# Second norm of a hybrid encoder layer: its small products a quarter of a block later in TensorE's order

## The chip, the cores and the metric

The kernel runs on one core of one Trainium2 chip, as one program. The metric is the device time of the execution in microseconds; the figure for a kernel is the median of its runs. The profile is of one further execution, taken by the hardware profiler. The engines are named as in the profile: PE is TensorE (its matmuls are called products here), PEld its weight loads, DVE is VectorE, ACT ScalarE, POOL GpSimd, SP SyncE, whose queue issues most DMAs.

## The reference

One encoder layer runs over two groups of tokens (2048 and 256) with the same weights; the width is 1024. The part that the change touches is in the second half of the layer: the output projection, its addition to the residual `x`, the second RMSNorm, and the start of the feed-forward part.

```python
def rmsnorm(x, w):
    y = x * lax.rsqrt(jnp.mean(x * x, axis=-1, keepdims=True) + EPS)
    return y * w

def encoder_layer(x, ...):
    h = rmsnorm(x, norm1_w)
    ... # mLSTM heads and attention heads on h @ w_in
    x = x + jnp.concatenate([m_out, a_out], axis=-1) @ w_out
    h = rmsnorm(x, norm2_w)
    u = centred_dwconv(h @ w_up, conv_w, conv_b)
    a, g = jnp.split(u, 2, axis=-1)
    return x + (jax.nn.silu(g) * a) @ w_down
```

A last RMSNorm follows. All is in float32.

## The kernel before, in words

The activations lie transposed on the chip: a tile has 128 of the 1024 channels in its partitions and tokens in its columns. A float32 operand is split in a high part and the rest (`fp32r`), and each product is made of three products of such parts.

The layer runs in phases. The first norm and the input projection come first; then the mLSTM heads, and with them and after them the attention heads. While the last attention blocks run, phase C (`phase_c`) makes the output projection, the residual and the second norm, block by block of 256 tokens. Phase U (`up_start`, `phase_u`) makes the first feed-forward product with a Strassen-like scheme of seven products, then the convolution and the gate; phase E the second feed-forward product and the last norm.

Phase C has nine blocks, taken in the order 0 to 6, 8, 7. A place in this order is called a turn here, turn 0 to turn 8. A turn has four quarters `z`, of 48 products each, and `mm` stops after each 12 of them (`k` is 0 to 3) so that a piece of attention can be put between: `phase_c` is a generator, and `run_both` steps it beside the attention's generator. The names in a turn are these:

- `cmx` is the projection's input, read from `mix_d` in HBM and split on ACT and DVE; `cx` is the residual, read from `xT` in HBM (L1060) into one of two buffers. `loads` issues both for the next turn after a turn's first quarter.
- `po` is a quarter's result in PSUM (two buffers); `post` adds it into `cx` on DVE (L1076), squares it on ACT (`csq`), and adds the squares up in `cacc` on POOL (L1082). `cacc` has one buffer.
- The norm's tail of a block stands in the next turn. `tail_a` folds `cacc` on POOL (L1085), then `rstd_cols` makes the small products of the sum with `ones` into `rs_c` (L135), takes the result on DVE (L138) and raises it to the power on POOL: `rcol_c` (L139). `tail_b` makes the small products of `rcol_c` with `ident` (L146), by which `rs_c` has a row of the factors in each partition, scales `cx` by `rs_c` on DVE (L1091) and stores the normed block to `n_d` in HBM (L1096).
- The last block's tail is `g.c_end`, called behind the first feed-forward unit's first two products.

The feed-forward part is done in two stretches of tokens, and a unit is two rows of 128 channels out of it. In the Strassen-like scheme the operands of the seven products are called "11", "21", "t2", "t1", "t3", "22" and "t4". "11", "21" and "22" (`n` in the rows) are quarters of the normed input, read from `n_d`; the `t` ones (`nt`) are differences of quarters, read from `n2t_d`. `n2_sums` makes these differences on POOL's queue, for a pair of channel tiles in two rounds (`rn`, two buffers): two loads from `n_d` (L1179), four subtractions (L1183), two stores to `n2t_d` (L1185). There are eight rounds for the first stretch of tokens; a pair is written into the code behind a quarter's `post`, from turn 5's second quarter on. `n2_load` (L1158 to L1160) loads an operand on SP in two pieces and splits it on ACT and DVE. `up_start` makes "11" into PSUM `pa` and "21" into `pb`; its function `rest` makes the other five. The weights `wu` and `wut` are split on ACT (L1221) and DVE.

What sets the order: each engine runs its own list, in the order that a scheduler gives at build time. While phase C runs beside attention, PE's list is in the order in which the code is written (`manual_schedule` for PE); the other engines' lists are sorted by the scheduler.

In the body, the remaining turns of phase C run without attention, with the loads of the first unit's operands put between:

```python
for _ in rest:
    if todo:
        todo.pop(0)()
for f in todo:
    f()
first = [up_start(g, s1, ..., ops, 0, NFC, rs)]
g.c_end()
```

Of the kernel before, what the change touches and what calls it, by code (L numbers as in the profile page):

```python
# [9 lines left out]
F32 = mybir.dt.float32  # L10
F32R = mybir.dt.float32r
AF = mybir.ActivationFunctionType
ALU = mybir.AluOpType
# [4 lines left out]
P = 128  # L18
D = 1024
NCC = D // P  # L20
# [6 lines left out]
NFC = FF // P  # L27
# [9 lines left out]
BT = 256  # L37
NB = T // BT
# [984 lines left out]
def phase_c(g, sn, sp, pp, wps):  # L1023

    nc = g.nc
    wo = ([], [])
    stage = []
    g.normed = set()  # L1030

    def weights(k, c):


        w = wps[k].tile([P, 2, 512], F32R, tag="w", name=f"wo{c}_{k}", bufs=WB)
        wo[k].append(w)
        if k == 0:
            t = g.raw.tile([P, 512], F32, tag="raw", name=f"ro{c}_{k}", bufs=2)
        else:
            if c % 4 == 0:  # L1040
                stage.append(sp.tile([P, 4, 512], F32, tag="x", name=f"ro{c}_{k}", bufs=2))
            t = stage[-1][:, c % 4]
        split(g, w[:, 0, :], w[:, 1, :], g.w_out[0, c * P:c * P + P, 512 * k:512 * k + 512], t)

    def loads(n, b):
        mx = []
        x = sp.tile([P, NCC, BT], F32, tag="x", name=f"cx{b}", bufs=2)
        for z in range(4):
            for o in range(2):
                c = 2 * z + o  # L1050
                if n and (n == 1 or n % 2 == 0):
                    m = sp.tile([P, 2, BT], F32R, tag="mx", name=f"cmx{b}_{c}", bufs=MXB)
                else:
                    m = sn.tile([P, 2, BT], F32R, tag="nT", name=f"cmx{b}_{c}", bufs=NTB)
                nc.sync.dma_start(f32(m[:, 1]), g.mix_d[b, :, c])
                nc.scalar.activation(m[:, 0], f32(m[:, 1]), AF.Copy)
                nc.vector.tensor_tensor(m[:, 1], f32(m[:, 1]), f32(m[:, 0]), ALU.subtract)  # L1057
                mx.append(m)
        for t in range(2):
            nc.sync.dma_start(x[:, :, t * P:(t + 1) * P], g.xT[2 * b + t])  # L1060
        return x, mx

    def mm(b, z, mx, po):

        for o in range(2):
            n = slice(((2 * z + o) % 4) * P, ((2 * z + o) % 4 + 1) * P)
            for c in range(NCC):
                for k, (a, h) in enumerate(((0, 0), (0, 1), (1, 0))):
                    nc.tensor.matmul(po[:, o], wo[z // 2][c][:, a, n], mx[c][:, h, :],  # L1069
                                     start=(c == 0 and k == 0), stop=(c == NCC - 1 and k == 2))  # L1070
                if c % 4 == 3:
                    yield

    def post(b, z, x, po, acc):
        xz = x[:, 2 * z:2 * z + 2]
        nc.vector.tensor_tensor(xz, po, xz, ALU.add)  # L1076
        if z % 2:
            g.st.dma_start(g.x1_d[:, 2 * z - 2:2 * z + 2, b * BT:(b + 1) * BT], x[:, 2 * z - 2:2 * z + 2])
        q = acc if z == 0 else sp.tile([P, 2, BT], F32, tag="sq", name=f"csq{b}_{z}", bufs=1)
        nc.scalar.activation(q, xz, AF.Square, scale=1.0 / 32.0)  # L1080
        if z:
            nc.gpsimd.tensor_tensor(acc, acc, q, ALU.add)  # L1082

    def tail_a(b, x, acc):
        nc.gpsimd.tensor_tensor(acc[:, 0], acc[:, 0], acc[:, 1], ALU.add)  # L1085
        return rstd_cols(g, sp, pp, [acc[:, 0]], BT, "r", f"c{b}")

    def tail_b(b, x, ps, r):
        r = rstd_rows(g, ps, r, BT)
        for z in range(NCC):  # L1090
            nc.vector.scalar_tensor_tensor(x[:, z], x[:, z], g.n2w[:, z:z + 1], r, ALU.mult, ALU.mult)  # L1091
            if z % 4 == 3:
                if b * BT < N2A:
                    g.st.dma_start(g.n2_d[0][:, z - 3:z + 1, b * BT:(b + 1) * BT], x[:, z - 3:z + 1])
                if b * BT >= N2B:
                    g.st.dma_start(g.n2_d[1][:, z - 3:z + 1, b * BT - N2B:(b + 1) * BT - N2B], x[:, z - 3:z + 1])  # L1096
        g.normed.add(b)

    for k in range(2):
        for c in range(NCC):  # L1100
            weights(k, c)
    sums = list(range(NCC // 2))

    order = (*range(NB - 2), NB - 1, NB - 2)
    nxt = loads(0, 0)
    yield None, C_LEAD
    prev = None
    for n, b in enumerate(order):
        x, mx = nxt
        for z in range(4):  # L1110
            if z == 1 and n + 1 < NB:
                yield 2 * order[n + 1], C_MM
                nxt = loads(n + 1, order[n + 1])
            po = pp.tile([P, 2, BT], F32, tag="po", name=f"po{b}_{z}")
            for k, _ in enumerate(mm(b, z, mx, po)):
                if z == 1 and k == 0 and prev is not None:
                    tail_b(*prev)
                if z < 3 or k < 3:
                    yield None, C_MM
            if z == 0:  # L1120
                if prev is not None:
                    prev = (*prev[0:2], *tail_a(*prev))
                acc = sp.tile([P, 2, BT], F32, tag="acc", name=f"cacc{b}", bufs=1)
            post(b, z, x, po, acc)
            if (n, z) > (5, 0) and sums:

                n2_sums(g, sp, 0, sums.pop(0), tag="rn", bufs=2)
        prev = (b, x, acc)

    def end():  # L1130
        tail_b(*prev[0:2], *tail_a(*prev))
    g.c_end = end

# [62 lines left out]
def banks(g, pool, name):  # L1198

    k = g.nbank = g.nbank + 1  # L1200
    return pool.tile([P, 2, 512], F32, tag=f"p{k % 2}", name=name, bufs=1)


def up_start(g, s1, bank, ops, b, jj, rs=None):


    nc = g.nc
    n = (DT[b + 1] - DT[b]) // 2
    m = n // 2
    nm = f"{b}_{jj}"  # L1210
    r1, r2 = rs or up_load(g, s1, b, jj)
    h = D // 2
    a11, a12, a21, a22 = r1[:, 0:h], r1[:, h:D], r2[:, 0:h], r2[:, h:D]
    t1, t2, t4 = (s1[0].tile([P, h], F32, tag="tmp", name=f"tw{k}_{nm}", bufs=3) for k in (1, 2, 4))

    def mul(p, k, src, add=False):

        i = g.nwu = (g.nwu + 1) % WU
        w = s1[i // 3].tile([P, 2, NCC // 2, P], F32R, tag="wu", name=f"wu{k}_{nm}", bufs=3 if i < 3 else WU - 3)
        hi, lo = (w[:, a].rearrange("p c n -> p (c n)") for a in range(2))  # L1220
        nc.scalar.activation(hi, src, AF.Copy)  # L1221
        nc.vector.tensor_tensor(lo, src, f32(hi), ALU.subtract)
        for z in range(2):
            for c in range(NCC // 2):
                for i, (aa, bb) in enumerate(((0, 0), (0, 1), (1, 0))):
                    nc.tensor.matmul(p[:, z], w[:, aa, c, :], ops[k][:, c, bb, z * m:z * m + m],  # L1226
                                     start=c == 0 and i == 0 and not add, stop=c == NCC // 2 - 1 and i == 2,
                                     skip_group_check=add)
    p1, p2 = bank("a" + nm)[:, :, 0:m], bank("b" + nm)[:, :, 0:m]
    mul(p1, "11", a11)  # L1230
    mul(p2, "21", a12)

    nc.gpsimd.tensor_tensor(t1, a21, a22, ALU.add)
    nc.gpsimd.tensor_tensor(t2, t1, a11, ALU.subtract)
    nc.gpsimd.tensor_tensor(a21, a11, a21, ALU.subtract)
    nc.gpsimd.tensor_tensor(t4, a12, t2, ALU.subtract)

    def rest(u1, u2):


        u11, u12, u21, u22 = (u[:, k * n:k * n + n].rearrange("p (z t) -> p z t", z=2) for u in (u1, u2) for k in range(2))

        def copy(o, p):
            nc.scalar.activation(o, p, AF.Copy)  # L1244

        def add(o, p, q):
            nc.vector.tensor_tensor(o, p, q, ALU.add)
        copy(u11, p1)
        add(u11, p2, u11)
        mul(p1, "t2", t2, True)  # L1250
        copy(u12, p1)
        p3 = bank("c" + nm)[:, :, 0:m]
        mul(p3, "t1", t1)
        copy(u21, p3)
        mul(p1, "t3", a21, True)
        add(u22, p1, u21)
        mul(p3, "22", t4, True)
        add(u12, p3, u12)
        mul(p1, "t4", a22, True)
        copy(u21, p1)  # L1260
    return rest
# [336 lines left out]
def body(tc, aps, phases="abcd"):  # L1598
# [5 lines left out]
    with ExitStack() as st:  # L1604
# [83 lines left out]
        with ExitStack() as s2:  # L1688
# [6 lines left out]
            g.nup, g.nwu = 0, -1  # L1695
            rs = up_load(g, s1, 0, NFC)
            todo = [lambda k=k: n2_load(g, ops, 0, k) for k in EARLY]
            for _ in rest:
                if todo:
                    todo.pop(0)()  # L1700
            for f in todo:
                f()

            first = [up_start(g, s1, lambda nm: banks(g, pd[(g.nbank + 1) // 2 % 2], "p" + nm), ops, 0, NFC, rs)]
            g.c_end()
            s_wo.close()
            pd.append(pool(s5, "d_v", bufs=1, space=PSUM))
            phase_u(g, tc, s1, pd, ops, first)
# [94 lines left out]
```

## Time and profile before

| | before |
|---|---|
| median of 3 runs (each) | 3371.0 us (3368.56, 3371.0, 3371.91) |
| span of the profiled execution | 3372.4 us |
| instructions | 57131 |
| busy PE, PEld | 97%, 90% |
| busy DVE, ACT, POOL | 71%, 53%, 39% |
| matmuls | 21366 |

The profiled execution's span is 1.4 us above the median of the runs. Busy time counts the time in which an engine works on an instruction; a wait for another engine or a DMA is idle time. In a row of the timeline stand the start, the length, the engine, the line, the operation, the tiles out and in, the shapes and the count of instructions put together in the row; behind it, in brackets, the idle time ahead of it on this engine and who ended it.

### The profile page before, as it was taken

The page shows a single profiled execution, that of the slowest core. Times are in us where ns is not written, and L with a number is a line of the kernel's source. Part 1 is how long each engine was busy: PE and PEld are TensorE (multiplying, and loading weights), DVE is VectorE, ACT ScalarE, POOL GpSimd, SP SyncE. Part 2 cuts the span into 40 slices and gives each one's busy share as a digit, 9 for nine tenths or more (in the row PEclk, how much of TensorE's full clock was granted, in tenths as well). Part 3 has the DMA queues.
Part 4 walks back from the last instruction along what each step waited for, and adds up shares of the span by engine and source line. Part 5 has one row for each costly group of instructions (what it writes and reads, how often), then busy time and mean ns, then how long its engine had stood idle before and what let it go on. Part 6 is the DMA issues. An engine that isn't in the chain of part 4 may idle for free. (4 is left out here: it accounts for less than half of the span.)

```text
span 3372.4 us, 57131 instructions
## 1 busy us (share of the span) xinstructions
PE 3271.5 (97%) x21366; PEld 3047.6 (90%) x21366; DVE 2403.1 (71%) x3727; ACT 1802.4 (53%) x3781; POOL 1327.6 (39%) x1686
## 2 busy tenths in 40 slices
PE   8899999999999999899999999999999999999998
PEld 6788888888888888788889999999999998999998
DVE  7875687777768788876766778877877776544573
ACT  5545666667666777665552544445555555323331
POOL 8652133213333323211246457645554442851112
PEclk9999999999999999999999999999999999999999
DMA  8765343343336444433347334424322223885563
GB/s 273 229 201 150 94 126 97 105 125 98 113 108 188 130 135 128 123 99 96 103 133 263 129 102 148 127 96 176 107 93 97 100 93 102 302 274 172 164 223 107
DMA packets 300636, 483.03 MB, mean 143 GB/s; under 512 B 36597, under 2 KB 186279, under 8 KB 300359
## 3 DMA queue, kind: packets, MB, share of 16 engines
q1 hardware_dynamic: 247543, 348.34, 32.8%
q0 software_dynamic: 36256, 121.60, 10.8%
q10 hardware_dynamic: 16560, 9.44, 0.9%
q8 instruction: 168, 2.75, 0.3%
q14 instruction: 109, 0.89, 0.1%
HBM read 337.37 MB, written 141.91 MB: 142 GB/s over the span
## 5 line engine op out<-in xcount | busy, mean ns | idle before, releaser
L622 DVE TENSOR_TENSOR pl<-ps,ph 128x512 fp32r<-128x512 f32 x520 | 354.0, 685 | 202.1 <-ACT ps L621 190.3
L1226 PE MATMUL pa<-nt,wut 128*128 128x290 f32 (+1 forms) x3168 | 449.2, 298 | 8.7 <-ACT u L1244 8.6
L620 ACT ACTIVATE ph<-ps 128x512 fp32r<-128x512 f32 x520 | 310.0, 596 | 265.7 <-PE ps L617 253.1
L1226 PEld LDWEIGHTS pa<-nt,wut 128*128 128x128 f32 x3168 | 433.1, 190 | 10.9 <-ACT u L1244 10.6
L591 DVE TENSOR_REDUCE mx<-px 128x1 f32<-128x512 f32 (+1 forms) x528 | 346.5, 674 | 100.0 <-PE px L590 98.0
L1336 DVE SCALAR_TENSOR_TENSOR y<-u,cw,y 128x1152 f32<-128x1152 f32 (+1 forms) x176 | 325.3, 1848 | 39.2 <-ACT yc L1334 17.5
L634 PE MATMUL pv<-ph,v 128*128 128x512 f32 (+1 forms) x1040 | 319.4, 402 | 0.8 <-ACT ph L620 0.3
L621 ACT ACTIVATE ps<-ps 128x512 f32<-128x512 f32 x520 | 310.3, 597 | 0.0
L1555 PE MATMUL et<-tet,wet 128*128 128x384 f32 x1584 | 279.0, 336 | 0.0
L1555 PEld LDWEIGHTS et<-tet,wet 128*128 128x128 f32 x1584 | 277.1, 188 | 0.0
L1069 PEld LDWEIGHTS po<-cmx,wo 128*128 128x128 f32 x1728 | 221.6, 191 | 9.6 <-DVE cmx L1057 1.5
L1069 PE MATMUL po<-cmx,wo 128*128 128x256 f32 x1728 | 225.8, 284 | 1.5 <-DVE cmx L1057 1.3
L1555 PE MATMUL e<-te,we 128*128 128x384 f32 x1188 | 213.9, 341 | 11.0 <-ACT te L1397 7.1
L1555 PEld LDWEIGHTS e<-te,we 128*128 128x128 f32 x1188 | 211.5, 191 | 12.0 <-ACT te L1397 7.3
L616 PE MATMUL ps<-qq,kk 128*128 128x512 f32 x520 | 215.9, 417 | 6.0 <-DVE mx L591 3.8
L780 PE MATMUL mj<-mn,wm 128*128 128x256 f32 x1296 | 200.8, 289 | 9.7 <-DMA mn<-n_d 3.9
L780 PEld LDWEIGHTS mj<-mn,wm 128*128 128x128 f32 x1296 | 185.5, 194 | 26.6 <-issue 6.8
L617 PE MATMUL ps<-qm,kl 65*128 65x512 f32 x520 | 207.6, 401 | 0.0
L590 PE MATMUL px<-kk,qq 128*128 128x512 f32 (+1 forms) x528 | 203.2, 415 | 3.9 <-DVE mx L591 2.6
L790 PEld LDWEIGHTS mv<-wm,mn 128*128 128x128 f32 x1296 | 181.9, 190 | 17.8 <-ACT qb L786 2.3
L790 PE MATMUL mv<-wm,mn 128*128 128x256 f32 x1296 | 194.8, 285 | 0.9 <-ACT qb L786 0.8
L634 PE MATMUL pv<-pl,v 128*128 128x512 f32 x520 | 192.2, 401 | 0.0
(307 smaller groups left out, 7216.9 us busy)
## 6 DMA issues: line engine op xcount, KB each, us to landing
mn<-n_d SPq DMA_DIRECT2D x216, 256.0 KB, 3.4
ru<-w_up SPq DMA_DIRECT2D x88, 512.0 KB, 3.6
a_d<-y POOLq DMA_DIRECT2D x88, 288.0 KB, 2.6
a_d<-tc POOLq DMA_DIRECT2D x66, 288.0 KB, 2.8
n_d<-n1T SPq DMA_DIRECT2D x18, 1024.0 KB, 5.7
dm<-nm_d POOLq DMA_DIRECT2D x72, 256.0 KB, 4.0
mjn<-n_d SPq DMA_DIRECT2D x72, 256.0 KB, 3.5
mvn<-n_d SPq DMA_DIRECT2D x72, 256.0 KB, 3.1
```

The costliest lines, as they stand in the source:

```text
L591: nc.vector.tensor_reduce(s.mx[:, t, z0:z0 + 1], ps[:, 0:w], AX.X, ALU.max)
L616: nc.tensor.matmul(ps, kk[:, kc:kc + P], s.qq[:, 0:N], start=True, stop=False)
L620: nc.scalar.activation(ph, ps, AF.Exp)
L621: nc.scalar.activation(ps, ps, AF.Exp)
L622: nc.vector.tensor_tensor(pl, ps, f32(ph), ALU.subtract)
L634: nc.tensor.matmul(s.pv[0:HD if k in (1, 3) else P, 0:N], v, p, start=(kp == 0 and k == 0), stop=(2 * kp + 2 == s.nk and k == 5))
L780: nc.tensor.matmul(pj[:, o], s.w[c][:, a, o * P:(o + 1) * P], nT[c][:, :, h, :], start=(c + o + k == 0), stop=(c == NCC - 1 and k == 2 and ...
L790: nc.tensor.matmul(pv[:, o], nT[c][:, o, a, :], s.w[c][:, h, 256:512], start=(c + o + k == 0), stop=(c == NCC - 1 and k == 2 and o == 1))
L1069: nc.tensor.matmul(po[:, o], wo[z // 2][c][:, a, n], mx[c][:, h, :], start=(c == 0 and k == 0), stop=(c == NCC - 1 and k == 2))
L1226: nc.tensor.matmul(p[:, z], w[:, aa, c, :], ops[k][:, c, bb, z * m:z * m + m], start=c == 0 and i == 0 and not add, stop=c == NCC // 2 - 1 ...
L1336: nc.vector.scalar_tensor_tensor(y[:, s:e], u[:, s + k:e + k], cw[:, k, jj:jj + 1], y[:, s:e], ALU.mult, ALU.add)
L1555: nc.tensor.matmul(ps[m // 2][:, m % 2], w[:, aa, m * P:(m + 1) * P], t[:, bb], start=p == 0 and n == 0, stop=p == NP - 1 and n == 2)
```

## The change

Four things are moved, and nothing of the layer's computation is changed:

- The tail of a block goes later in the next turn: the fold stays behind the first quarter's squares (now into a tile of its own, `cfold`, so that `cacc` is free), the `ones` products go from the end of quarter 0 to the half of quarter 1, the `ident` products and the scaling from the first 12 products of quarter 1 to the half of quarter 2.
- The loads of the next `cx` from `xT` are split off from `loads` (now `residual`) and stand behind this tail.
- The first `n2_sums` is written one quarter later, and the loads of the first unit's operands begin only when all `n2_sums` are written.
- The last block's `c_end` has two parts: the `ones` products stand between "11" and "21", the `ident` products behind "21". Its sum is not folded: four `ones` products add up both halves of `cacc`. The last addition of squares goes from POOL to DVE. PE's list follows the code's order here too (`manual_schedule`), where before the scheduler set it.

```diff
     def loads(n, b):
         mx = []
-        x = sp.tile([P, NCC, BT], F32, tag="x", name=f"cx{b}", bufs=2)
...
+        return mx
+
+    def residual(b):
+        x = sp.tile([P, NCC, BT], F32, tag="x", name=f"cx{b}", bufs=2)
         for t in range(2):
             nc.sync.dma_start(x[:, :, t * P:(t + 1) * P], g.xT[2 * b + t])
-        return x, mx
+        return x
...
         if z:
-            nc.gpsimd.tensor_tensor(acc, acc, q, ALU.add)
+            (nc.vector if b == order[-1] and z == 3 else nc.gpsimd).tensor_tensor(acc, acc, q, ALU.add)
 
     def tail_a(b, x, acc):
-        nc.gpsimd.tensor_tensor(acc[:, 0], acc[:, 0], acc[:, 1], ALU.add)
-        return rstd_cols(g, sp, pp, [acc[:, 0]], BT, "r", f"c{b}")
+        return rstd_cols(g, sp, pp, acc, BT, "r", f"c{b}")
+
+    def fold(b, x, acc):
+        s = sp.tile([P, BT], F32, tag="fold", name=f"cfold{b}", bufs=1)
+        nc.gpsimd.tensor_tensor(s, acc[:, 0], acc[:, 1], ALU.add)
+        return b, x, [s]
...
-        x, mx = nxt
+        mx = nxt
...
             for k, _ in enumerate(mm(b, z, mx, po)):
-                if z == 1 and k == 0 and prev is not None:
-                    tail_b(*prev)
+                if prev is not None and z == 1 and k == 1:
+                    prev = (*prev[0:2], *tail_a(*prev))
+                if z == 2 and k == 1:
+                    if prev is not None:
+                        tail_b(*prev)
+                    if n + 1 < NB:
+                        xn = residual(order[n + 1])
                 if z < 3 or k < 3:
                     yield None, C_MM
             if z == 0:
                 if prev is not None:
-                    prev = (*prev[0:2], *tail_a(*prev))
+                    prev = fold(*prev)
...
-            if (n, z) > (5, 0) and sums:
+            if (n, z) > (5, 1) and sums:
...
-    def end():
-        tail_b(*prev[0:2], *tail_a(*prev))
-    g.c_end = end
+    def end_a():
+        b, x, acc = prev
+        g.c_rows = (b, x, *tail_a(b, x, [acc[:, 0], acc[:, 1]]))
+    g.c_end = (end_a, lambda: tail_b(*g.c_rows))
...
-def up_start(g, s1, bank, ops, b, jj, rs=None):
+def up_start(g, s1, bank, ops, b, jj, rs=None, between=()):
...
     mul(p1, "11", a11)
+    for f in between[0:1]:
+        f()
     mul(p2, "21", a12)
+    for f in between[1:]:
+        f()
...
-            for _ in rest:
-                if todo:
-                    todo.pop(0)()
...
+            with tc.manual_schedule(engines={mybir.EngineType.PE}):
+                for _ in rest:
+                    if todo and not g.sums:
+                        todo.pop(0)()
...
+                first = [up_start(g, s1, lambda nm: banks(g, pd[(g.nbank + 1) // 2 % 2], "p" + nm), ops, 0, NFC, rs,
+                                  g.c_end)]
```

In the rows of the engines' lists below a name ends in a number of its own for each tile; lines are those of the kernel in question (L1226 of before is L1241 of after, L1179 is L1194, L1185 is L1200, L1183 is L1198, L1082 is L1085, L1085 is L1092).

PE, from the end of turn 8 into the first feed-forward unit (`pa_22` and `pb_22`; `wu` with `n_0_22390` is "11", with `n_0_22391` "21", `wut` with `nt_0_22392` "t2"; `pc_22` is "t1"). Before:

```order
L1226 MATMUL pa_22_23073<-n_0_22390,wu_0_22_23075 128x290 x10
L1226 MATMUL pb_22_23074<-n_0_22391,wu_0_22_23102 128x290 x24
L1226 MATMUL pa_22_23073<-nt_0_22392,wut_0_22_23229 128x290 x6
L135 MATMUL rs_c_23134<-ones,cacc_22894 128x2 x2
L1226 MATMUL pa_22_23073<-nt_0_22392,wut_0_22_23229 128x290
L146 MATMUL rs_c_23134<-ident,rcol_c_23137 128x128 x2
L1226 MATMUL pa_22_23073<-nt_0_22392,wut_0_22_23229 128x290 x17
L1226 MATMUL pc_22_23257<-nt_0_23199,wut_0_22_23258 128x290 x2
```

After:

```order
L1241 MATMUL pa_22_23083<-n_0_22355,wu_0_22_23085 128x290 x24
L135 MATMUL rs_c_23112<-ones,cacc_22898 128x2 x4
L1241 MATMUL pb_22_23084<-n_0_22356,wu_0_22_23120 128x290 x24
L1241 MATMUL pa_22_23083<-nt_0_22357,wut_0_22_23241 128x290 x6
L146 MATMUL rs_c_23112<-ident,rcol_c_23117 128x128 x2
L1241 MATMUL pc_22_23269<-nt_0_23211,wut_0_22_23270 128x290 x24
L1241 MATMUL pa_22_23083<-nt_0_22357,wut_0_22_23241 128x290 x18
```

The `ones` products went from behind "21" to ahead of it and are four, the `ident` products stand 30 products behind them instead of 1, and "t1" (`pc_22`) now stands ahead of the last 18 products of "t2". The other 14 products of "11", which before were put singly into turns 7 and 8, stand here now.

POOL, from the seventh round's end (`rn_3_0`) to the last `rcol_c`. Before:

```order
L1185 DMA n2t_d<-rn_3_0_1_22278 128x2x290
L1179 DMA rn_3_1_0_22286<-n_d_61 128x2x290
L139 TENSOR_TENSOR rcol_c_22891<-rcol_c_22891,mhalf 128x2
L1179 DMA rn_3_1_1_22288<-n_d_61 128x2x290
...
L1185 DMA n2t_d<-rn_3_1_1_22288 128x2x290
L1082 TENSOR_TENSOR cacc_22894<-cacc_22894,csq_1_22960 128x512
L1082 TENSOR_TENSOR cacc_22894<-cacc_22894,csq_2_23013 128x512
L1082 TENSOR_TENSOR cacc_22894<-cacc_22894,csq_3_23067 128x512
L1085 TENSOR_TENSOR cacc_22894<-cacc_22894 128x256
L139 TENSOR_TENSOR rcol_c_23137<-rcol_c_23137,mhalf 128x2
```

After:

```order
L1085 TENSOR_TENSOR cacc_22898<-cacc_22898,csq_2_23023 128x512
L1198 TENSOR_TENSOR rn_3_0_1_22421<-rn_3_0_1_22421,rn_3_0_0_22419 128x290
L1200 DMA n2t_d<-rn_3_0_0_22419 128x2x290
L1198 TENSOR_TENSOR rn_3_0_1_22421<-rn_3_0_1_22421 128x290
L1200 DMA n2t_d<-rn_3_0_1_22421 128x2x290
L139 TENSOR_TENSOR rcol_c_23117<-rcol_c_23117,mhalf 128x2
L1194 DMA rn_3_1_0_22429<-n_d_61 128x2x290
L1194 DMA rn_3_1_1_22431<-n_d_61 128x2x290
```

The eighth round (`rn_3_1`) stood ahead of the last block's squares (`cacc_22894`); now it stands behind the last block's `rcol_c`, and the seventh round stands between that block's squares.

POOL, around the `rcol_c` of turn 6 (`rcol_c_22270` before, `rcol_c_22387` after; `o` is a block of attention's output). Before, and then after:

```order
L1185 DMA n2t_d<-rn_1_1_0_22057 128x2x290
L1183 TENSOR_TENSOR rn_1_1_1_22059<-rn_1_1_1_22059 128x290
L1185 DMA n2t_d<-rn_1_1_1_22059 128x2x290
L139 TENSOR_TENSOR rcol_c_22270<-rcol_c_22270,mhalf 128x2
L1179 DMA rn_2_0_0_22169<-n_d_61 128x2x290
```

```order
L1200 DMA n2t_d<-rn_1_1_0_22164 128x2x290
L655 TENSOR_TENSOR o_14_22333<-o_14_22333,rs_14_22334 64x512
L139 TENSOR_TENSOR rcol_c_22387<-rcol_c_22387,mhalf 128x2
L1198 TENSOR_TENSOR rn_1_1_1_22166<-rn_1_1_1_22166 128x290
L1085 TENSOR_TENSOR cacc_22253<-cacc_22253,csq_1_22416 128x512
```

Here it stood behind the fourth round's second store (`rn_1_1`); now it stands behind that round's first store, and behind attention's last `o`.

More of the change, by code (lines that the diff above doesn't have):

```diff
@@ L1101, in phase_c @@
             weights(k, c)
-    sums = list(range(NCC // 2))
+    sums = g.sums = list(range(NCC // 2))
     order = (*range(NB - 2), NB - 1, NB - 2)
     nxt = loads(0, 0)
+    x = residual(0)
     yield None, C_LEAD
@@ L1121, in phase_c @@
                 if prev is not None:
-                    prev = (*prev[0:2], *tail_a(*prev))
+                    prev = fold(*prev)
                 acc = sp.tile([P, 2, BT], F32, tag="acc", name=f"cacc{b}", bufs=1)
             post(b, z, x, po, acc)
-            if (n, z) > (5, 0) and sums:
+            if (n, z) > (5, 1) and sums:
                 n2_sums(g, sp, 0, sums.pop(0), tag="rn", bufs=2)
         prev = (b, x, acc)
-    def end():
-        tail_b(*prev[0:2], *tail_a(*prev))
-    g.c_end = end
+        x = xn
+    def end_a():
+        b, x, acc = prev
+        g.c_rows = (b, x, *tail_a(b, x, [acc[:, 0], acc[:, 1]]))
+    g.c_end = (end_a, lambda: tail_b(*g.c_rows))
 OPS = ("11", "21", "t2", "t1", "t3", "22", "t4")
@@ L1697, in body @@
             todo = [lambda k=k: n2_load(g, ops, 0, k) for k in EARLY]
-            for _ in rest:
-                if todo:
-                    todo.pop(0)()
[L1701 to L1705, printed above, removed]
+            with tc.manual_schedule(engines={mybir.EngineType.PE}):
+                for _ in rest:
+                    if todo and not g.sums:
+                        todo.pop(0)()
+                for f in todo:
+                    f()
+                first = [up_start(g, s1, lambda nm: banks(g, pd[(g.nbank + 1) // 2 % 2], "p" + nm), ops, 0, NFC, rs,
+                                  g.c_end)]
             s_wo.close()
```

## The prediction

> **What bounds the kernel now.** I read the page first (busy times, table 2), then windows by stage, then who TensorE (PE) waited for between 1440 and 1910 us, then the timelines of PE, GpSimd (POOL) and the queues at those places. Views in this order: page part 1; windows; waits of PE.
>
> ```profile
> PE 3271.5 (97%) x21366; PEld 3047.6 (90%) x21366; DVE 2403.1 (71%) x3727; ACT 1802.4 (53%) x3781; POOL 1327.6 (39%) x1686
> ...
> 1500.00:1900.00 400.00, 385.88 (x2561) 349.77 (x2561) 267.14 (x423) 192.12 (x354) 136.66 (x143) 0.98 0.44 143
> 1900.00:3372.00 1472.00, 1442.48 (x9886) 1438.85 (x9885) 1009.81 (x891) 644.31 (x979) 678.78 (x645) 0.99 0.43 145
> ...
> PE rs_c L146 <- POOL rcol_c L139: 5.6, 2, 2.8
> PE rs_c L135 <- POOL cacc L1085: 2.1, 2, 1.8
> PE pc L1226 <- ACT wut L1221: 1.3, 1, 1.3
> PE pa L1226 <- ACT u L1244: 1.1, 2, 0.5
> ```
>
> PE is busy 97% of the span, so PE's own time is the bound, and only what PE waits for can be won. In the window 1500 to 1900, where phase C runs, PE lacks 14.1 us of 400 (columns: length, then busy time and instructions of PE, its weight loads, DVE, ACT, POOL, then the clock, the DMAs' share and GB/s). The columns of the waits are the sum, the number and the longest: the norm's small products (`rs_c`) account for 5.6 + 2.1 us, and a wait for `wut`, which stands on ScalarE (ACT) behind a copy of an unfinished sum, for 1.3. That is all that the change can take away directly.
>
> PE's timeline shows where (start, length, then the idle time before it and who ended it):
>
> ```profile
> 1760.96 3.01 PE L1069 MATMUL po<-cmx,wo 128*128 128x256 f32 x24
> 1765.78 0.61 PE L135 MATMUL rs_c<-ones,cacc 128*128 128x2 f32 x4 [1.81 <-POOL cacc L1085]
> ...
> 1772.45 23.15 PE L1069 MATMUL po<-cmx,wo 128*128 128x256 f32 x193
> ...
> 1805.60 1.07 PE L146 MATMUL rs_c<-ident,rcol_c 128*128 128x128 f32 x4 [2.81 <-POOL rcol_c L139]
> 1806.32 9.78 PE L1069 MATMUL po<-cmx,wo 128*128 128x256 f32 x69
> ...
> 1842.83 3.42 PE L1226 MATMUL pb<-n,wu 128*128 128x290 f32 x24
> 1846.09 0.96 PE L1226 MATMUL pa<-nt,wut 128*128 128x290 f32 x6
> ...
> 1850.80 1.22 PE L146 MATMUL rs_c<-ident,rcol_c 128*128 128x128 f32 x4 [2.84 <-POOL rcol_c L139]
> 1851.67 4.45 PE L1226 MATMUL pa<-nt,wut 128*128 128x290 f32 x17
> 1857.38 0.85 PE L1226 MATMUL pc<-nt,wut 128*128 128x290 f32 x2 [1.26 <-ACT wut L1221]
> ...
> 1858.55 3.96 PE L1226 MATMUL pc<-nt,wut 128*128 128x290 f32 x22
> ...
> 1806.00:1808.00 2.00, 2.00 (x12) 2.00 (x11) 2.00 (x4) 1.50 (x3) 1.74 (x2) 0.50 1.09 383
> 1851.00:1854.00 3.00, 3.00 (x14) 3.00 (x15) 1.95 (x5) 0.00 (x0) 0.00 (x0) 0.50 0.00 0
> ```
>
> The last two rows are windows; their PEclk of 0.50 says that after each wait of 2.8 us PE ran at half clock for a while. 193 products in 23.15 us are 0.120 us each; the 69 after the second wait took 9.78 instead of 8.28 (1.5 lost). 24 products of the feed-forward part take 3.42 (0.1425 each); the 17 after the last wait took 4.45 instead of 2.42 (2.0 lost), and the 26 from 1857.38 to 1862.51 took 5.13 instead of 3.71 (1.4 lost). So the waits cost 9.0 us and the clock after them 4.9.
>
> **What the change takes away.** Turns 0 to 8 are the blocks in their order. A quarter is 48 products, 5.76 us. Every sum of squares gets half a quarter more before PE asks for it, and between the `ones` and the `ident` products of a tail, where its power must come, stand 48 products instead of 12. At turns 6, 7 and 8 that covers one small step of DVE and one of POOL for `rcol_c` (0.16 and 0.74 below). In the last tail the products of "11" and "21" (3.4 us each) stand in front. The wait for `wut` goes as the weights' copies now stand ahead of the copy that waits. Taken away: 9.0 + 4.9 = 13.9 us. The 14 products of "11" that filled places in turns 7 and 8 move to the end: no net. Last squares: one add of 1.3 us on POOL becomes one on DVE, and two more small products cost PE about 0.3 (the row of four at 1765.78 took 0.61). The separate `cfold` takes the same POOL time as the fold in place.
>
> **What it moves onto the path.** The second norm feeds `n2_sums`, the Strassen differences of the normed blocks, done on POOL's queue in order, by DMA from and to HBM; their results are the operands t2, t1 and t3 of the first feed-forward unit. Two things move. The norm of block 4 (on which the second to eighth rounds of sums rest) is now done at the half of turn 5's third quarter, not the first quarter of its second; and each round stands between POOL's steps of later turns: the sixth to eighth, which before were over when turn 8's second square came, now stand behind it, the eighth behind the last `rcol_c`.
>
> POOL's and DVE's timeline of before, turn 5 to turn 6:
>
> ```profile
> 1722.57 3.21 DVE L1091 SCALAR_TENSOR_TENSOR cx<-cx,nw,rs_c 128x256 f32<-128x256 f32 x8
> 1734.13 1.60 PE L1069 MATMUL po<-cmx,wo 128*128 128x256 f32 x12
> 1735.63 3.38 DVE L651 RECIPROCAL rs<-rs 64x128 f32<-64x128 f32 x4 [1.22 <-ACT rs L643]
> ...
> 1727.80 0.78 POOL L1179 DMA_DIRECT2D rn<-n_d  x1 [9.49 <-DMA n_d<-cx]
> 1733.42 0.74 POOL L1179 DMA_DIRECT2D rn<-n_d  x1 [4.84 <-ACT ph L620]
> 1745.35 0.76 POOL L1179 DMA_DIRECT2D rn<-n_d  x1
> 1756.84 0.73 POOL L1179 DMA_DIRECT2D rn<-n_d  x1 [1.65 <-DMA n2t_d<-rn]
> 1769.73 0.74 POOL L139 TENSOR_TENSOR rcol_c<-rcol_c,mhalf 128x2 f32<-128x2 f32 x1
> ...
> 1744.12 1.30 POOL L655 TENSOR_TENSOR o<-o,rs 64x512 f32<-64x512 f32 x1
> 1752.65 0.77 POOL L1185 DMA_DIRECT2D n2t_d<-rn  x1
> ...
> 1766.43 0.16 DVE L138 TENSOR_SCALAR rcol_c<-rs_c 128x2 f32<-128x2 f32 x1 [1.72 <-PE rs_c L135]
> ...
> DMA to landing us min/median/max: 2.7/3.9/6.7
> DMA to landing us min/median/max: 2.7/4.2/9.5
> ```
>
> First new wait, turn 6. The scale by `rs_c` (L1091) began at 1722.57; the round's first load began 5.2 later, when the stores had landed. Now PE makes `rs_c`'s rows after the product row of 1734.13, and on DVE the scale stands behind the reciprocals of 1735.63 + 3.38, so it starts near 1739.0 and the load near 1744.2. From this load to turn 6's `rcol_c` on POOL stand three rounds, as before. Before they took 1769.73 - 1727.80 = 41.9, which gives 1786.1 and, with its 0.74, 1786.8: the upper end. A clean round took 1756.84 - 1745.35 = 11.5; two of them, a third up to its first store (1753.42 - 1745.35 = 8.1), the product `o` (1.3) and `rcol_c` (0.74) give 1777.3: the lower end. PE asks for it after turn 6's first quarter ended (1763.97), two pieces of attention, 72 products (8.64) and `rs_c` (0.46). The two pieces are what stands from 1765.78 to 1772.45 besides 22 products (2.64) and the norm's own (0.93): 3.1. That makes 1776.2, so PE waits between 1.1 and 10.6 us. I take 5.0: the first round had 6 us more than a clean one while `xT` loads ran, and those loads again follow the same stores. With it 1.5 us of half clock, as after the wait at 1805.
>
> Second new wait, first unit. PE's row is now: 24 of "11", four `rs_c`, 24 of "21", 6 of t2, two rows of `rs_c`, then t1, whose operand's second half needs the eighth round. Its chain was, before, on POOL, SP, ACT and DVE:
>
> ```profile
> 1826.56 0.75 POOL L1179 DMA_DIRECT2D rn<-n_d  x1
> 1830.85 1.59 POOL L1183 TENSOR_TENSOR rn<-rn,rn 128x290 f32<-128x290 f32 x2 [1.70 <-DMA rn<-n_d]
> 1832.38 0.74 POOL L1185 DMA_DIRECT2D n2t_d<-rn  x1
> ...
> 1838.24 2.70 SPq L1158 DMA_DIRECT2D nt<-n2t_d  x3
> ...
> 1843.03 1.16 ACT L1159 ACTIVATE nt<-nt 128x1160 fp32r<-128x1160 f32 x1
> ...
> 1844.22 1.50 DVE L1160 TENSOR_TENSOR nt<-nt 128x1160 fp32r<-128x1160 f32 x1 [1.82 <-ACT nt L1159]
> ```
>
> From the second load's issue to the end of the low part 1845.72 - 1826.56 = 19.2 us. It used to end before the rows of 1850.80 let PE need it. Now the first load is issued when the last `rcol_c` leaves POOL, the second 0.75 later: 19.9 after `rcol_c` is the upper end; with the shortest landings of the two tile rows (2.7 for load and for store, in place of 4.3 and 5.9) 15.1 is the lower. I take 18.0, nearer to the measured piece since the last norm's stores and the operands' loads run beside it again. `rcol_c` ends 1.0 after `rs_c` (DVE 0.16, POOL 0.74). PE has from `rs_c` on 3.26 + 0.79 + 0.36 + 0.8 (6 of t1) = 5.2 us of work. Wait: 1.0 + 18.0 - 5.2 = 13.8 (10.9 to 15.7), then 2.0 of slow clock as after 1850.80. The second half of t2 and operand "22" follow on the same queues, 1.5 us apart on DVE, PE takes 2.4 to 2.6 for each piece of 18: no further wait. The two waits for `u` (1.1) go, as loads come no later than before while PE is later.
>
> Loads of `x`: each is issued later on SP behind the norm's stores; PE notices only when two `po` banks are full, 14.4 + 5.8 = 20 us after the rows of `rs_c`. Before, the last one let DVE go on 18.5 us after the rows of 1805.60:
>
> ```profile
> 1824.10 0.69 DVE L1076 TENSOR_TENSOR cx<-po,cx 128x512 f32<-128x512 f32 x1 [7.27 <-DMA cx<-xT]
> ```
>
> So 0, at most 2. Other queues (the mix loads of turn 8 now stand behind t2's first half on SP) have as much room: 0.
>
> **Sum**, from the end of turn 6's first quarter: -13.9 + 0.3 + (5.0 + 1.5) + (13.8 + 2.0) - 1.1 = +7.6. The profiled span is 3372.4, 1.4 above the median of the three times (3371.0): span 3380.0, median 3378.6.
>
> A rule against these two waits: each of these waits is mostly DMA latency; the rows say 3.9 and 4.2 us at the median from issue to landing. The Trainium skill, "DMA: Bandwidth & Descriptors", section "Anatomy of one DMA — SWDGE (gpsimd) path", puts a GpSimd-issued DMA at about 2.0 us plus bytes over 436 GB/s, which for 290 KB is an estimate of 2.7 us, so its sum would be the one of the second rival below. The trace has that value only as its minimum.
>
> **Rivals.**
> - The waits go and nothing takes their place: -13.9 + 0.3 - 1.1, span 3357.7, median 3356. It needs the eighth round ready 5.2 us after the last `rcol_c`; POOL's order, where the round's first load stands behind that very step, and the 19.2 us of the chain speak against it. Chance 0.11.
> - Short landings (2.7 for loads and stores throughout): turn 6 does not wait, the last wait is 1.0 + 15.1 - 5.2 = 10.9: -13.9 + 0.3 + 10.9 + 2.0 - 1.1 = -1.8, median 3369.2. For it: the minima in the tile rows; against: the store of 1832.38 let the load go only 5.9 us later. Chance 0.17.
> - A third wait: the turn-8 `x` or mix loads come late, PE stands in turn 8, up to 3 us, with no clock lost: median 3381.6. Chance 0.10.
>
> **How the numbers follow.** The forecast's case has 0.62; its ends are +0.6 (waits of 1.1 and 10.9) and +15.1 (10.6 and 15.7). What a measurement can tell from no change is 0.2%, 6.7 us, here, so slower begins at 3377.7. Of the 0.62 I put 0.36 above it and 0.26 within. Slower 0.36 + 0.10 = 0.46; same 0.26 + 0.13 (of the short landings) = 0.39; faster 0.11 + 0.04 = 0.15. The range 3364 to 3387 leaves out the first rival and the very top. The forecast's own range is 3372 to 3386.
>
> **What would show it.** Right: PE waits for `rcol_c` once, at turn 6's third quarter (1 to 11 us), and once for `nt`, in t1, for 11 to 16 us; the other `rs_c` waits and that for `wut` are gone; POOL's eighth round starts after its last `rcol_c`. Wrong: t1's operand is there within 5 us of the rows of `rs_c` (then some 14 us are won), or turns 7 and 8 show waits for `po`, `cmx` or `cx`.

## The result, and the profile after

The changed kernel takes 3381.9 us at the median of its four runs (3381.1 to 3386.9), the kernel before 3369.8 in the runs of the same comparison: a ratio of 1.0039, 95% interval 1.0027 to 1.0051. Timed again beside later experiments it gave 1.0034 (1.0022 to 1.0046). So the change costs 7 to 17 us, about 12. Two runs of one kernel can differ by 10 us and more (before: 3362 to 3378 in one set), so a profile's span is compared with another's stage by stage below, and whole times only by these ratios.

The profile after is of an execution of 3382.1 us with a span of 3380.4. First line of part 1 of its page, then who PE waited for between 1700 and 1920 us (sum, number, longest):

```profile
PE 3271.6 (97%) x21370; PEld 3049.5 (90%) x21370; DVE 2411.3 (71%) x3728; ACT 1801.6 (53%) x3781; POOL 1329.8 (39%) x1684
...
PE pc L1241 <- ACT nt L1174: 6.2, 1, 6.2
PE rs_c L146 <- POOL rcol_c L139: 4.0, 1, 4.0
PE pc L1241 <- DVE wut L1237: 3.8, 1, 3.8
PE ps L616 <- DVE mx L591: 2.6, 1, 2.6
PE rs_c L135 <- DVE cacc L1085: 1.3, 1, 1.3
PE po L1072 <- DVE cx L1079: 0.9, 1, 0.9
PE pc L1241 <- DVE nt L1175: 0.8, 1, 0.8
```

PE's busy time is what it was, to 0.1 us; the change only moved waits. The waits of turn 7 and of the last `ident` products are gone; one of 4.0 stands at turn 6, and in the first unit's t1 (`pc`) one of 3.8 + 6.2 + 0.8 = 10.8. PE's timeline after, at the places shown of before:

```profile
1772.23 0.50 PE L135 MATMUL rs_c<-ones,cfold 128*128 128x2 f32 x4
...
1782.53 0.85 PE L146 MATMUL rs_c<-ident,rcol_c 128*128 128x128 f32 x4 [4.00 <-POOL rcol_c L139]
1783.03 18.91 PE L1072 MATMUL po<-cmx,wo 128*128 128x256 f32 x144
...
1846.94 1.04 PE L135 MATMUL rs_c<-ones,cacc 128*128 128x2 f32 x8 [1.29 <-DVE cacc L1085]
1847.84 4.98 PE L1241 MATMUL pb<-n,wu 128*128 128x290 f32 x24
...
1854.06 0.54 PE L1241 MATMUL pc<-nt,wut 128*128 128x290 f32 x2
1858.38 1.33 PE L1241 MATMUL pc<-nt,wut 128*128 128x290 f32 x4 [3.79 <-DVE wut L1237]
1865.92 0.61 PE L1241 MATMUL pc<-nt,wut 128*128 128x290 f32 x1 [6.21 <-ACT nt L1174]
1867.33 4.47 PE L1241 MATMUL pc<-nt,wut 128*128 128x290 f32 x17 [0.79 <-DVE nt L1175]
...
1899.90 0.43 PE L1241 MATMUL pa<-n,wu 128*128 128x290 f32 x2
```

The last row is the start of the third unit (the third pair of rows of 128 channels), the same product as in this row of before:

```profile
1889.87 0.43 PE L1226 MATMUL pa<-n,wu 128*128 128x290 f32 x2
```

From the end of turn 6's first quarter (1763.97 before, 1766.74 after) to that product lie 125.9 us before and 133.2 after: 7.3 more, with the same products between, but for two more `ones` products. POOL's timeline after shows why t1 waits (its first row, an addition of squares, is taken up further below):

```profile
1844.12 1.29 POOL L1085 TENSOR_TENSOR cacc<-cacc,csq 128x512 f32<-128x512 f32 x1
...
1848.52 0.83 POOL L139 TENSOR_TENSOR rcol_c<-rcol_c,mhalf 128x2 f32<-128x2 f32 x1
1849.32 0.75 POOL L1194 DMA_DIRECT2D rn<-n_d  x1
...
1858.06 0.73 POOL L1200 DMA_DIRECT2D n2t_d<-rn  x1 [0.30 <-POOL rn L1198]
```

The eighth round begins as the last `rcol_c` leaves POOL (1849.35). Its last store is issued at 1858.06, the operand's loads follow on SP, its copy on ACT comes at 1864.70, and t1 has its whole operand at 1867.33, 18.0 us after `rcol_c`.

The rest of the +8.0 between the two spans is a sum of several pieces. Attention's last seven blocks each have one row of `pr` products; from the first such row to the last, these rows say 274.7 us before and 278.9 after:

```profile
1447.11 0.56 PE L605 MATMUL pr<-identr,m4r 128*128 128x128 f32 x4
1721.83 0.64 PE L605 MATMUL pr<-identr,m4r 128*128 128x128 f32 x4
...
1444.91 0.66 PE L605 MATMUL pr<-identr,m4r 128*128 128x128 f32 x4 [0.16 <-DVE m4r L599]
1723.80 0.56 PE L605 MATMUL pr<-identr,m4r 128*128 128x128 f32 x4
```

That is a loss of 4.2 us in a stage of which the prediction had not spoken; from its last row to the end of turn 6's first quarter 0.8 more went. Some 4 us came back: 2.2 ahead of this stage (its first row stands at 1444.91 instead of 1447.11), and 2.0 behind the start of the third unit, from which to the end of the span it is 1482.5 us before and 1480.5 after. Both pieces hold the same products in both kernels. In the profiles of all kernels below, the second piece takes between 1479.6 and 1485.4 us, so a few us there say nothing about the change.

### The profile page after: what moved, and what is told of

Read it like the earlier page. It is cut to its first block, busy times and chain, and to the rows that moved or that the text cites. A ratio compares the mean times of both kernels' runs of the same rounds, so it can differ in the third digit from the quotient of the medians.

```text
span 3380.4 us, 57143 instructions
## 1 busy us (share of the span) xinstructions
PE 3271.6 (97%) x21370; PEld 3049.5 (90%) x21370; DVE 2411.3 (71%) x3728; ACT 1801.6 (53%) x3781; POOL 1329.8 (39%) x1684
## 3 DMA queue, kind: packets, MB, share of 16 engines
q0 software_dynamic: 36256, 121.60, 10.9%
## 5 line engine op out<-in xcount | busy, mean ns | idle before, releaser
L1241 PE MATMUL pa<-nt,wut 128*128 128x290 f32 (+1 forms) x3168 | 444.6, 296 | 5.0 <-ACT u L1263 4.8
L1241 PEld LDWEIGHTS pa<-nt,wut 128*128 128x128 f32 x3168 | 429.7, 189 | 6.6 <-ACT u L1263 6.0
```

## The experiments

Theory A is the prediction's: the new waits come from the place of `n2_sums` on POOL's queue. Theory B: they come from the norm's own lateness. Theory C arose from the rows above: the change loses in the attention stage. Theory D arose from the first run: the splitting of operands on DVE stands ahead of urgent work there. Each ratio is against the kernel before, timed beside the kernel in question.

**Undoing the change by turns.** A condition `late` chooses between the new place of the tail and the `x` load and the old one:

```diff
+            late = n > 5
...
+                if not late:
+                    xn = residual(order[n + 1])
...
+                if not late and prev is not None and z == 1 and k == 0:
+                    tail_b(*prev)
-                if prev is not None and z == 1 and k == 1:
+                if late and prev is not None and z == 1 and k == 1:
                     prev = (*prev[0:2], *tail_a(*prev))
-                if z == 2 and k == 1:
+                if late and z == 2 and k == 1:
...
+                    if not late:
+                        prev = (*prev[0:2], *tail_a(*prev))
...
-            if (n, z) > (5, 1) and sums:
+            if (n, z) > (5, 0) and sums:
```

> The quarter-later tail only at turns 6 to 8; turns 0 to 5 as before, and the first n2_sums written a quarter earlier, as before; the new end stays. On POOL the eighth round stands ahead of the last rcol_c again. Theory A (the change's cost is the sums' place on POOL): the wait for nt in the first unit falls from 10.8 us to under 3, the turn-6 wait for rcol_c to 0 to 4, and the waits of before (2.81, 2.84, 1.26, with their half clock 13.9 in all) stay away: 6 to 13 us faster than before. Theory B (the t1 wait comes from the last norm standing so late, whatever the sums do): nt still waits some 10 us, no faster than before. Theory C (what the change lost it lost in the attention stage): about 5.6 us less than the changed kernel, nt still waits.

Measured: 1.0048 (1.0032 to 1.0063), 16 us slower than before. The wait for `nt` is gone, as A has it, and the wait for `rcol_c` at turn 6 is 4.4, just above A's 0 to 4; but the time is a miss. Who PE waited for in this kernel between 1764 and 1910 us, then DVE's and SP's timelines there, and how long the load of the last row took to land:

```profile
PE po L1072 <- DVE cx L1079: 9.3, 1, 9.3
PE pa L1248 <- ACT u L1270: 4.5, 2, 2.3
PE rs_c L146 <- POOL rcol_c L139: 4.4, 1, 4.4
...
1800.32 2.58 DVE L1182 TENSOR_TENSOR n<-n 128x1160 fp32r<-128x1160 f32 x1 [3.05 <-ACT n L1181]
...
1804.77 3.71 DVE L1182 TENSOR_TENSOR n<-n 128x1160 fp32r<-128x1160 f32 x2
1808.39 1.35 DVE L1182 TENSOR_TENSOR nt<-nt 128x1160 fp32r<-128x1160 f32 x1
1809.67 0.68 DVE L1079 TENSOR_TENSOR cx<-po,cx 128x512 f32<-128x512 f32 x1
...
1789.99 2.92 SPq L1180 DMA_DIRECT2D n<-n_d  x4
...
1793.54 1.46 SPq L1063 DMA_DIRECT2D cx<-xT  x1
DMA to landing us min/median/max: 13.8/13.8/13.8
```

With the sums done a quarter earlier, the operand loads are written earlier too, and DVE's list has all five low parts (L1182; the rows show four of them) ahead of turn 7's first addition (1809.67). They wait for their copies on ACT, both `po` buffers stay full, and PE stands for 9.3 us. Theory D puts the wait down to this list. But on SP, too, the second half of turn 7's residual (1793.54) stands behind the five operand loads, and it lands 13.8 us later, at 1807.3. With DVE's list free of low parts the addition could have come 2.3 us earlier at most; for the rest of the 9.3 the load had not landed.

The converse, `late = n <= 5` with the sums as in the changed kernel:

> The converse: the quarter-later tail at turns 0 to 5 only, sums a quarter later as in the changed kernel, turns 6 to 8 as before, the new end. The eighth round's loads stand ahead of the last rcol_c on POOL. Theory A: nt waits less than in the changed kernel (3 to 9 us), the waits at turns 6 and 7 of before (some 5 us and their clock) are back: within 4 us of before. Theory C: the attention stage loses its 5.6 us here too: that much slower than the kernel with the late tails from turn 6 on, by this stage alone.

Measured: 1.0061 (1.0046 to 1.0076). A miss for A, which had 3 to 9 us for `nt` and a time within 4 us of before: the eighth round's loads stand ahead of the last `rcol_c`, but so late that t2 waits 10.8 + 0.8 us for `nt`, and turn 7's `ones` products wait 7.9 for the fold, which stands behind a round on POOL. The attention stage took 281.7 us by the same rows, as C said.

`late = False`, the sums as before, the new end alone (with `cfold`, and with the operand loads still begun only when all sums are written):

> Only the new end (ones between 11 and 21, ident behind 21, last addition on DVE, PE's list in the code's order); all tails of turns 0 to 8 and the sums as before. Theory A: the last tail's waits (0.17, 2.84, 1.26 and 3.4 of half clock, 7.7 in all) go, nothing new comes since the eighth round stands ahead of the last rcol_c; turns 6 and 7 keep their 4.9 us of waits: 5 to 8 us faster than before. Rival: the t1 product, which now stands ahead of the rest of t2, waits for its operand anyway (over 5 us): no change.

Measured: 1.0003 (0.9992 to 1.0014), no gain: a miss for A. The rival has the time but not the reason, as t1 does not wait for its operand. No wait for `rcol_c` stands in the last tail. But the wait for `wut` (1.3) stays, and a new one comes: 3.2 us ahead of the product of "22" (`pc<-n,wu`), because the copy that empties `pc` stands on ACT behind operand copies that wait for their loads.

`late = n > 4`, the rest as changed:

> As the changed kernel, but the tails of turns 0 to 4, which stand beside attention, as before. From turn 5 on all lists are those of the changed kernel. Theory A: nt waits 10 to 12 us and rcol_c of turn 6 about 4, as in the changed kernel. Theory C (the late tail's scaling on DVE holds up attention's max and sums): 3 to 6 us faster than the changed kernel. If the attention stage's 5.6 us were an accident of one profile: within 2 us of the changed kernel.

Measured: 1.0039 (1.0024 to 1.0054). The waits from turn 6 on are the changed kernel's (3.4 for `rcol_c`; 3.4 + 9.1 + 0.8 in t1). The attention stage took 273.3 us, 5.6 less than after, yet the ratio does not show it, as the expectation's last reading, an accident of one profile, had said.

**POOL's rounds themselves.** In the changed kernel, the eighth round's loads and subtractions are left out, and then the whole round is done twice:

```diff
+        if b == 0 and c == 3 and z == 1:
+            for k in range(2):
+                nc.gpsimd.dma_start(g.n2t_d[b, k, :, c, :, z * m:z * m + m], rs[k])
+            continue
```

```diff
-    for z in range(2):
+    for v, z in enumerate((0, 1, 1) if b == 0 and c == 3 else (0, 1)):
```

> The changed kernel without the eighth round's loads and subtractions: its place in n2t_d is filled with the seventh round's results instead (this part of the sums is left out of the computation), so the last store of sums is issued 1.5 us behind the last rcol_c instead of 9.4. Theory A (POOL's eighth round behind the last rcol_c makes the t1 wait): the wait for nt goes from 7.0 us to 0 to 1, that for wut on DVE (3.8) may stay; with less half clock 6 to 10 us faster than the changed kernel, so within 5 us of before. Theory B (the last norm's own lateness or the operands' loads make it): within 2 us of the changed kernel. The turn-6 wait (4.0) and the attention stage are as in the changed kernel under both.

> The changed kernel with the eighth round done twice (the second time stores the same values). Theory A: the wait for nt grows by one round, 9 to 12 us: 9 to 13 us slower than the changed kernel. Theory B: the ninth round lies beside other waits: under 3 us slower.

Measured: 1.0018 (1.0008 to 1.0027) without the round and 1.0067 (1.0053 to 1.0081) with one more, against 1.0034 to 1.0039 with one: 5 to 7 us faster, 9 to 11 slower. Who PE waited for, without the round, then with one more:

```profile
PE pc L1246 <- ACT wut L1241: 6.7, 1, 6.7
...
PE pc L1241 <- ACT nt L1174: 18.4, 1, 18.4
```

One round more adds 12.2 us to the wait for `nt` (6.2 to 18.4), without it the wait is gone. The wait for `rcol_c` at turn 6 is 3.8 in both. So A holds for t1 and B falls. Part of the gain is lost to `wut` (6.7 where 3.8 was expected), whose copy now stands on ACT behind two `nt` copies that wait for their loads.

**The fourth round**, left out in the same way (`c == 1`), for turn 6:

> The changed kernel without the fourth round's loads and subtractions (its place is filled with the third round's results; this part of the sums is left out). Theory A: POOL has one round less ahead of turn 6's rcol_c, so the wait there falls from 4.0 us to 0 to 2; all later rounds come earlier too, the eighth stands ahead of the last rcol_c, and the wait for nt falls under 3 us: 8 to 15 us faster than the changed kernel. Rival (turn 6's wait comes from attention's last product o or its DVE steps, not from the sums): rcol_c still waits about 4 us.

Measured: the wait for `rcol_c` at turn 6 fell to 1.6 and `nt` to 1.2 in all, as A has it. The time did not follow: 1.0046 (1.0033 to 1.0059), no faster than the changed kernel (1.0034 beside it), where 8 to 15 us faster was expected. Turn 7 shows two new waits; the last row is DVE's, the addition for which the first of them waited:

```profile
PE po L1072 <- DVE cx L1079: 6.4, 1, 6.4
PE rs_c L135 <- POOL cfold L1092: 3.3, 1, 3.3
...
1808.23 1.29 DVE L1079 TENSOR_TENSOR cx<-po,cx 128x512 f32<-128x512 f32 x2 [1.40 <-DMA cx<-xT]
```

The low parts stand ahead of this addition here too, but DVE was done with them and idle for 1.4 us when turn 7's residual landed. This load is issued at 1800.54, behind the operand loads and the mix loads on SP. So this wait ends with the late load, not with the low parts on DVE's list.

**Theory D.** To the kernel with `late = n > 5`, and to one with `late = n > 6`, is added a gate on the operand loads (16 and 12 pieces):

```diff
-                for _ in rest:
-                    if todo and not g.sums:
+                for i, _ in enumerate(rest):
+                    if todo and not g.sums and i >= 16:
```

> As the kernel with the late tails from turn 6 on and the sums begun as before, but the first unit's operand loads are written a third of a turn (16 pieces of 12 products, counted from attention's end) later, which puts DVE's splitting of 11 and 21 behind turn 7's first two additions to cx. Theory D (that kernel's 9.3 us wait for cx is DVE splitting operands whose copies on ACT and loads on SP come late, ahead of the addition): the wait for cx falls under 2 us and the run is 8 to 13 us faster than that kernel, so within 5 us of before. Rival (the x load itself is late): the wait stays over 5 us and the time within 3 us of that kernel.

> Late tails at turns 7 and 8 only, sums as before, the new end, operand loads 12 pieces later. Turn 6 keeps its old tail and its 1.8 us wait. Theories A and D together: no wait of 4 us for rcol_c in turn 6, none for nt, none over 2 us for cx; what is left at the start of the first unit (wut on DVE, u on ACT) costs 2 to 6 us: 2 to 9 us faster than before. If it is no faster, the waits are only handed on to the next list (DVE or ACT) again.

Measured: 1.0001 (0.9992 to 1.001) and 1.0004 (0.9994 to 1.0015). With 16 pieces the wait for `cx` fell from 9.3 to 0.3 us, and the ratio by 0.0047, 16 us: the early operand loads made the wait. Theory D and its rival, the late residual, are not told apart by this, since the gate changes SP's order as well. The second half of the residual is now issued ahead of the operand loads, 6.5 us earlier than without the gate:

```profile
1787.02 0.83 SPq L1063 DMA_DIRECT2D cx<-xT  x1
```

The rows of the ungated kernel speak for the load (all but 2.3 of the 9.3 us). In the gated one t2 now waits 6.4 + 0.8 for its operand, which is loaded late, and `rcol_c` 5.2 at turn 6. With `late = n > 6` no wait of more than 3.5 us is left; there are seven kinds of small ones (3.7 `cx`, 3.5 `u`, 2.1 the fold, 1.3 `wut`), and it is no faster than before: a miss. No version beat the kernel before.

**Theory C by itself**, `late = n <= 4`, the sums and turns 5 to 8 as before, the new end:

> The kernel with only the new end, and the quarter-later tail (and x load) at turns 0 to 4 alone, which stand beside attention; turns 5 to 8 and the sums as before. Theory C (the late x load and stores collide with the mix loads, whose copies stand ahead of attention's work on ACT and DVE): from the first to the last pr product of the seven attention blocks 277 to 282 us, as in the four kernels with late tails there, not 270 to 275; 4 to 7 us slower than the kernel with only the new end. Rival (accident of the profiles): 270 to 275 us, and the same time as that kernel.

Measured: 1.0025 (1.0016 to 1.0035), against 1.0003 without late tails: 7 us slower, and the stage took 278.8 us. That is the size which C had. Its rows, and those of the kernel with the new end alone:

```profile
1445.33 0.66 PE L605 MATMUL pr<-identr,m4r 128*128 128x128 f32 x4 [0.25 <-DVE m4r L599]
1724.15 0.64 PE L605 MATMUL pr<-identr,m4r 128*128 128x128 f32 x4
...
1442.82 0.56 PE L605 MATMUL pr<-identr,m4r 128*128 128x128 f32 x4
1714.66 0.64 PE L605 MATMUL pr<-identr,m4r 128*128 128x128 f32 x4
```

Over all kernels profiled, the stage takes 277.4 to 281.7 us in the seven profiles with late tails at turns 0 to 4, and 270.0 to 274.7 in the six without. Where the last loss (2.6 us for `mx`) comes from, the queues show: POOL's timeline before, then after, then SP's wait and the timelines of SP, DVE and PE after:

```profile
1688.16 0.73 POOL L1185 DMA_DIRECT2D n2t_d<-rn  x1
...
1699.10 1.15 POOL L658 DMA_DIRECT2D mix_d<-o  x2
...
1695.80 1.59 POOL L1198 TENSOR_TENSOR rn<-rn,rn 128x290 f32<-128x290 f32 x2 [2.52 <-DMA rn<-n_d]
1697.35 1.28 POOL L655 TENSOR_TENSOR o<-o,rs 64x512 f32<-64x512 f32 x1
...
1701.26 1.12 POOL L658 DMA_DIRECT2D mix_d<-o  x2
...
SPq L1054 <- DMA mix_d<-o: 2.7, 1, 2.7
...
1690.98 1.27 SPq L1063 DMA_DIRECT2D cx<-xT  x2
1699.28 7.26 SPq L1054 DMA_DIRECT2D cmx<-mix_d  x8
...
1707.77 0.43 DVE L1056 TENSOR_TENSOR cmx<-cmx 128x256 fp32r<-128x256 f32 x1 [2.10 <-ACT cmx L1055]
...
1711.41 0.79 PE L616 MATMUL ps<-qq,kk 128*128 128x512 f32 x1 [2.62 <-DVE mx L591]
```

The first round of sums rests on the norm whose tail stands in turn 4. Before, this round had left POOL (1688.16) when attention's `o` came. With the tail a quarter later the round is later too, and `o` and its store into `mix_d` stand between the round's steps. SP's last mix load waits 2.7 us for this store, DVE's splits of `cmx` wait for that load by way of ACT, attention's maxima (`mx`) stand behind them, and PE waits for these. SP has this wait, 1.5 to 2.7 us, in all seven profiles with late tails there and in none of the six without. So it is theory A's mechanism, at a turn that the prediction left out. The `x` load, whose collision with the mix loads theory C had named, is later too, but it landed 6.3 us after its issue, ahead of the first mix load; the rows do not show that collision. This chain is read from the rows; leaving out the first round was not tried. The other loss, 1.6 us for `m4r` behind the eight scalings on DVE, is in all kernels with late tails there.

**The changed kernel once more:**

> The changed kernel once more, beside the other two on the same chip. All theories: 3380 to 3384 us, nt waits 6 to 8 us behind wut, rcol_c of turn 6 about 4.

Measured: 3379.6 us median (3376.4 to 3384.7), with `nt` 6.7, `rcol_c` 5.5, `wut` 3.4. So the wait at turn 6 differs by 1.5 us between two profiles of one kernel.

## Why the prediction was right, point by point

- **The sum.** From the end of turn 6's first quarter +7.6 was forecast, the two profiles say +7.3. The span was forecast at 3380.0 and was 3380.4. The agreement of the span is partly luck: the attention stage lost 4.2, and about as much came back in pieces whose products the change does not touch, all of it outside the sum. The whole time moved by about 12 us, some 4 more than forecast, and lies in the range. The low end of the forecast's case, put at +0.6, is +0.8 by its own terms (1.1 and 10.9 in place of 5.0 and 13.8).
- **What goes.** The waits of 0.26, 2.81, 0.17 and 2.84 went, and so did the two for `u`. The wait for `wut` did not go: on DVE it stands behind the eight scalings of the last norm and waits 3.8. It cost nothing of its own, since the operand's second half came later still; in four kernels whose operand comes early (the new end alone, tails late from turn 7 on, tails late at turns 0 to 4, the fourth round left out) it is 1.3, as before.
- **Turn 6.** 4.0 for a forecast of 5.0 (1.1 to 10.6), and 144 products in 18.91 us instead of 17.28: 1.6 of half clock, 1.5 forecast. The cause, the rounds ahead on POOL, was shown by leaving one out: 1.6, where the five profiles of kernels that have this round and the changed order from turn 5 on say 3.4 to 5.5.
- **First unit.** From the last `rcol_c` to the end of the low part 18.0 us were forecast and 18.0 measured; the wait was 10.8, not 13.8, since PE came 3 us later to it. About half of this is "21", which takes 4.98 instead of 3.42 behind a wait that the prediction had at nothing. The last add on DVE needs a square that waits on ACT for POOL's earlier add (1844.12); this add stands between the steps of the seventh round, so the `ones` products wait 1.3 us. The other half is the first seven products of t1, between the waits: 0.54 + 1.33 + 0.61 us, at half clock, where 0.8 was reckoned for six. The wait is 3.0 shorter than forecast, the 1.3 and the 1.6 of "21" are not in the sum: the slips cancel, by luck.
- **The `x` loads.** 0, at most 2, was forecast for the turns after attention; 0.9 was measured, at turn 8. In kernels with other orders of the operand loads a late residual cost much more (the 6.4, and most of the 9.3).
- **What failed.** The step that began the sum at turn 6. Turns 0 to 5 were given no term, although their tails, their `x` loads and the first round of sums move too: the runs show 7 us there (1.0025 against 1.0003), as a stage 277.4 to 281.7 against 270.0 to 274.7. The comparison of the changed kernel with its tails of turns 0 to 4 put back (1.0039, 1.0024 to 1.0054, against 1.0034) does not show this gain in the whole time. In its profile the stage's 5.6 us were there, and the third unit began at 1891.88, 8.0 us earlier than after; but from there to the end it took 1485.4 us, the longest of all profiles, against 1480.5. What lengthens this stretch, whose products are the same in both, stays open.
- **The rivals.** The waits did not go without a successor, and landings were not short: the median for `rn` between 1700 and 1880 us was 4.7 us (2.7 to 7.8), 4.0 before, further from the estimate of 2.7 by the Trainium skill's rule (worked out in the prediction from "DMA: Bandwidth & Descriptors", section "Anatomy of one DMA — SWDGE (gpsimd) path"). The third wait, for `cx`, did come in turn 8, at 0.9, by the late load that this rival has.
- **Its own signs.** The eighth round did start behind the last `rcol_c`, and `rcol_c` was waited for once, at turn 6. But the wait in t1 was 10.8, just under the 11 to 16 named; the wait for `wut` stayed, the `ones` products of the last tail got a new one, and a wait for `cx`, named as a sign of being wrong, came at 0.9.

## What to carry to other kernels

A step that is moved later takes its whole queue along: ask, for each engine's list, what stood behind it and now stands ahead of something urgent, and begin the sum at the first place that moves, not at the first that waits. When a wait is taken away and the time stays, look at the next list for the operation that now comes first and waits for a load: here the wait went from POOL's sums to the operand loads, to ACT's copies and back. Before naming a list as the cause, look at what landed last: a load that is late on SP looks, from PE, just like an addition that is late on DVE. Doing a suspected round twice and not at all is a cheap proof; it gave the round's price here (12.2 us of wait) although single runs scatter by 10 us.

## What the runs showed that was not expected

The wait moves among the lists almost without loss: four kernels with quite different waits (the new end alone, both gated ones, and before) lie within 0.0004 of one ratio, each known to about 0.001.

And a wait of only 1.3 us was followed by half clock: the 24 products of "21" behind it took 4.98 us instead of 3.42, and the first window below says 0.66 for the granted clock (last numbers: clock, DMA share, GB/s). The second window stands behind a longer wait, the 1.8 us ahead of turn 6's `ones` products in the kernel before, and there the clock stayed full:

```profile
1847.80:1852.80 5.00, 5.00 (x28) 5.00 (x28) 0.76 (x2) 0.00 (x0) 3.13 (x5) 0.66 0.48 143
...
1765.80:1770.80 5.00, 4.97 (x34) 4.39 (x35) 0.16 (x1) 0.63 (x1) 4.58 (x7) 1.00 0.29 102
```

The Trainium skill, "TensorE: Matmul & The Clock Gate", puts the limit in its section "Why this matters for your kernels" at gaps of about 3 us. By the measurement, gaps of 1.3 and 2.8 us can suffice, but one of 1.8 us did not, so the length of a gap alone does not decide; what else does, these runs do not show.
